# Causal mask of an attention on VectorE, in place of matmuls with the identity

## The chip, the cores and the metric

The kernel is one launch on one core of a Trainium2 chip. The core has TensorE (PE, with a weight load, PEld, ahead of each matmul), VectorE (DVE), ScalarE (ACT), GpSimd (POOL) and SyncE (SP, which issues most of the DMAs here). The metric is the device time of one execution in microseconds; smaller is better. The median of three runs of the kernel before is 1168.8 us (1168.61 to 1170.69).

## The reference

One decoder block on 512 tokens of width 1024 in float32: a SwiGLU half step, a mixing stage, and a second SwiGLU half step. The mixing stage holds a gated MLP over chunks, and a causal differential attention with 8 heads, each with two maps (m = 0, 1) of query and key dimension 64. This is the part that the change touches:

```python
s = jnp.einsum('bhmqd,bhmkd->bhmqk', qb, kf)        # qb: 128 queries, already times 64 ** -0.5
mask = kpos[None, :] <= qpos[:, None]
p = jax.nn.softmax(jnp.where(mask, s, -jnp.inf), axis=-1)
a = p[:, :, 0] - lam * p[:, :, 1]
return jnp.einsum('bhqk,bhkd->bhqd', a, vf)
```

## The kernel before

Activations lie feature by token in tiles of 128 partitions by 512 tokens. Every float32 product is made of three matmuls on operands that are split in two parts: ScalarE casts a tile to the fp32r part `hi` and VectorE subtracts it from the tile to get `lo` (`split`, L138 to L140). Weights come in 512 KB loads on the SP queue into `w_raw`, are split into `w_hi` and `w_lo` (three buffers each in the mixing stage), and each of these chunks feeds one "unit" of 24 matmuls of 512 columns. `pump(n)` runs n units, and starts the load and the split of the next one ahead of the matmuls of the present one.

Between the two SwiGLU parts the program runs a fixed sequence of steps, one for each head h and each block i of 128 queries, 32 in all. A step is `scores(h, i)`, then `pump` of 0 to 2 units by the table `UNITS`, then jobs of earlier steps: `turn_weights` of the step two before (`LAG = 2`) transposes the weights of the softmax and splits them into `at_hi` and `at_lo`, `attend` multiplies them with the values at the end of a head, `mean_square` and `subnorm` normalize the result, `turn` transposes the queries and keys of the next heads, `gate_values` does the gated MLP. The order on each engine is then set by a scheduler that works with costs of its own, so what is written as one step is interleaved with its neighbours.

`scores(h, i)` works on w = 128 (i + 1) keys, so on tiles of 128 by 128 up to 128 by 512. Each map takes one PSUM bank of the pool `att`, which has four; all the transposes, `attend`, `mean_square` and `gate_values` use the same four. Per map there are two matmuls of w columns (L669, L670: the two halves of the contraction hold the parts of queries and keys) and one of 128 columns (L671) that multiplies the identity `ident_r` with the mask `mask_r` and adds -2^100 above the diagonal of the last block. VectorE then takes the negated maximum of each row (L676), ScalarE takes the exponential out of PSUM with this as bias, and the row's sum with it (L677). Reciprocal, scaling and the difference of the two maps follow on VectorE and ScalarE (L680 to L683), in SBUF tiles of the pool `scratch`, which has six.

The two constants are made in `mixing_constants`, which is run inside the first SwiGLU part. The same function scales `qk_col`, the column by which `turn` multiplies the queries.

Of the kernel before, what the change touches and what calls it, by code (L numbers as in the profile page):

```python
# [13 lines left out]
F32 = mybir.dt.float32  # L14
F32R = mybir.dt.float32r
I32 = mybir.dt.int32
AF = mybir.ActivationFunctionType
ALU = mybir.AluOpType
AX = mybir.AxisListType

P = 128
T = 512
# [8 lines left out]
QK = 64  # L31
# [2 lines left out]
LN_EPS = 1e-5  # L34
LAM_INIT = 0.8 - 0.6 * math.exp(0.0)
ROPE_THETA = 500000.0
MASK = -(2.0**100)
RINT = 12582912.0
TWO_PI_A = 6.28125
TWO_PI_B = 2029.0 / 2**20  # L40
# [18 lines left out]
def decoder_block(  # L59
# [25 lines left out]
    nc = tc.nc  # L85
# [6 lines left out]
    small = ctx.enter_context(tc.tile_pool(name="small", bufs=4))  # L92
# [3 lines left out]
    def bank(pool=acc):  # L96
        return pool.tile([P, T], F32, name="bank_" + pool.name, tag=pool.name)
# [7 lines left out]
    def scratch():  # L105
        return tmp.tile([P, T], F32, name="scratch", tag="scratch")
# [37 lines left out]
    ident = const.tile([P, P], F32, name="ident")  # L144
# [257 lines left out]

    mc = ctx.enter_context(tc.tile_pool(name="mc", bufs=1))
    nr = ROT // 2
    ident_r = mc.tile([P, P], F32R, name="ident_r")
    mask_r = mc.tile([P, P], F32R, name="mask_r")
    sub_gain = mc.tile([P, 1], F32, name="sub_gain")
    qk_col = mc.tile([P, 2], F32, name="qk_col")
    neg_lam = mc.tile([P, 1], F32, name="neg_lam")
# [2 lines left out]
    rot2 = mc.tile([P, NT, 2, 2, nr], F32, name="rot2")  # L412

    def mixing_constants():
        nc.vector.tensor_copy(ident_r, ident)
        mask = scratch()[:, :P]
        nc.gpsimd.memset(mask, 0.0)
        nc.gpsimd.affine_select(
            out=mask, in_=mask, compare_op=ALU.is_ge, fill=MASK, base=0, pattern=[[-1, P]], channel_multiplier=1
        )  # L420
        nc.vector.tensor_copy(mask_r, mask)
        c = 3 * KD
        nc.vector.tensor_scalar(sub_gain, gains[:, c : c + 1], LAM_INIT - 1.0, None, op0=ALU.mult)
        nc.vector.tensor_copy(qk_col, gains[:, c + 1 : c + 3])
        nc.vector.tensor_scalar(qk_col[:, 0:1], qk_col[:, 0:1], QK**-0.5, None, op0=ALU.mult)


        s = scratch()
        lam = s[:, : 4 * QK].rearrange("p (a b d) -> p a b d", a=2, b=2)
        lp = s[:, 4 * QK : 6 * QK].rearrange("p (n d) -> p n d", d=QK)  # L430
        le = s[:, 6 * QK : 6 * QK + 2]
        nc.gpsimd.dma_start(out=s[:, : 4 * QK].rearrange("p (n d) -> p n d", d=QK), in_=lam_row.partition_broadcast(P))
        nc.vector.tensor_tensor(lp, lam[:, :, 0, :], lam[:, :, 1, :], op=ALU.mult)
        nc.vector.tensor_reduce(le, lp, axis=AX.X, op=ALU.add)
        nc.scalar.activation(le, le, AF.Exp)
        nc.vector.tensor_tensor(neg_lam, le[:, 1:2], le[:, 0:1], op=ALU.subtract)
        nc.vector.tensor_scalar(neg_lam, neg_lam, -LAM_INIT, None, op0=ALU.add)


        s = scratch()  # L440
        n = NT * nr
        ang, turn, red, sin, cos = (
            s[:, i * n : (i + 1) * n].rearrange("p (t d) -> p t d", d=nr) for i in range(5)
        )
        gain = s[:, 5 * n : 5 * n + 2 * ROT].rearrange("p (q d) -> p q d", d=ROT)
        pos_f = s[:, 7 * n : 7 * n + NT]
        pos_i = small.tile([P, NT], I32, name="pos_i")
        nc.gpsimd.dma_start(out=pos_i, in_=pos)
        nc.gpsimd.dma_start(out=gain, in_=qk_row.partition_broadcast(P))
        nc.vector.tensor_copy(pos_f, pos_i)  # L450
        for i in range(nr):
            inv = float(np.float32(ROPE_THETA ** (-2.0 * i / ROT)))
            nc.vector.tensor_scalar(ang[:, :, i], pos_f, inv, None, op0=ALU.mult)
        for dst, quarter in ((sin, 0.0), (cos, 0.25)):
            nc.vector.tensor_scalar(turn, ang, 1.0 / (2.0 * math.pi), quarter, op0=ALU.mult, op1=ALU.add)
            nc.vector.tensor_scalar(turn, turn, RINT, None, op0=ALU.add)
            nc.vector.tensor_scalar(turn, turn, -RINT, None, op0=ALU.add)
            nc.vector.scalar_tensor_tensor(red, turn, -TWO_PI_A, ang, op0=ALU.mult, op1=ALU.add)
            nc.vector.scalar_tensor_tensor(red, turn, -TWO_PI_B, red, op0=ALU.mult, op1=ALU.add)
            nc.vector.scalar_tensor_tensor(red, turn, -TWO_PI_C, red, op0=ALU.mult, op1=ALU.add)  # L460
            if quarter:
                nc.vector.tensor_scalar(red, red, math.pi / 2.0, None, op0=ALU.add)
            nc.vector.tensor_scalar(red, red, PI32, -PI32, op0=ALU.min, op1=ALU.max)
            nc.scalar.activation(dst, red, AF.Sin)
        for q in range(2):
            g1 = gain[:, q, 0:nr].unsqueeze(1).to_broadcast([P, NT, nr])
            g2 = gain[:, q, nr:ROT].unsqueeze(1).to_broadcast([P, NT, nr])
            nc.vector.tensor_tensor(rot1[:, :, 0, q, :], cos, g1, op=ALU.mult)
            nc.vector.tensor_tensor(rot1[:, :, 1, q, :], sin, g1, op=ALU.mult)
            nc.vector.tensor_tensor(rot2[:, :, 0, q, :], sin, g2, op=ALU.mult)  # L470
            nc.vector.tensor_tensor(rot2[:, :, 1, q, :], cos, g2, op=ALU.mult)


    with tc.tile_pool(name="ff1", bufs=1) as ff1:
        xt = [residual.tile([P, T], F32, name=f"x0_{j}", tag="x") for j in range(KD)]

        def load1(k):
            nc.sync.dma_start(out=xt[k], in_=x[:, k, :])
            normed_input(k, xt[k], 0)

        def prepare1():
            nc.vector.tensor_scalar(neg_gains, gains[:, : 3 * KD], -1.0, None, op0=ALU.mult)
            for j in range(KD):
                add_squares(j, xt[j], latest["hi"])
            norm_scale()

        def constants1():
            with tc.issue_after(latest["hi"].ins), tc.issue_after(latest["lo"].ins):
                mixing_constants()

        def finish1(j, y):
            normed_input(j, y, 1)
            add_squares(j, y)
            nc.gpsimd.dma_start(out=x1_dram[j], in_=y)

        def again1(t, i):
            nc.sync.dma_start(out=t, in_=x[:, 2 * i : 2 * i + 2, :])

        ffn(ff1, gu1, dn1, 0, xt, finish1, load1, {0: prepare1, 5: constants1}, again1)
# [3 lines left out]
    with ExitStack() as mix:  # L503
        half = mix.enter_context(tc.tile_pool(name="half", bufs=PIECES))
        big = mix.enter_context(tc.tile_pool(name="big", bufs=1))

        def piece(name, dtype=F32R):
            return half.tile([P, T], dtype, name=name, tag="piece")
# [152 lines left out]
        heads_out = {}  # L661

        def scores(h, i):
            qd, ql, kd = turned[h]
            w = (i + 1) * P
            qs = slice(i * P, w)
            s = [bank(att)[:, :w] for _ in range(2)]
            for m in range(2):
                nc.tensor.matmul(s[m], lhsT=qd[m][:, qs], rhs=kd[m][:, :w], start=True, stop=False)  # L669
                nc.tensor.matmul(s[m], lhsT=ql[m][:, qs], rhs=kd[m][:, :w], start=False, stop=False)  # L670
                nc.tensor.matmul(s[m][:, qs], lhsT=ident_r, rhs=mask_r, start=False, stop=True)  # L671
            nmx = small.tile([P, 2], F32, name="nmx")
            den = small.tile([P, 2], F32, name="den")
            p = [scratch() for _ in range(2)]
            for m in range(2):
                nc.vector.tensor_reduce(nmx[:, m : m + 1], s[m], axis=AX.X, op=ALU.max, negate=True)  # L676
                nc.scalar.activation(  # L677
                    p[m][:, :w], s[m], AF.Exp, bias=nmx[:, m : m + 1], accum_out=den[:, m : m + 1]
                )
            nc.vector.reciprocal(den, den)  # L680
            nc.vector.tensor_tensor(den[:, 1:2], den[:, 1:2], neg_lam, op=ALU.mult)
            nc.scalar.activation(p[1][:, :w], p[1][:, :w], AF.Copy, scale=den[:, 1:2])
            nc.vector.scalar_tensor_tensor(  # L683
                p[0][:, :w], p[0][:, :w], den[:, 0:1], p[1][:, :w], op0=ALU.mult, op1=ALU.add
            )
            probs[h, i] = p[0]
# [252 lines left out]
        for step in range(max(jobs) + 1):  # L939
            if step < H * NT:  # L940
                scores(*divmod(step, NT))
                pump(UNITS[step // 8][step % 8])
            for work in jobs.get(step, []):
                work()
# [102 lines left out]
```

## Time and profile before

| | us |
|---|---|
| median of three runs | 1168.8 |
| lowest, highest run | 1168.61, 1170.69 |
| the profiled execution | 1167.13 |
| its span on the core | 1165.4 |
| steps of the attention | about 445 to 700 of the span |

The profile is of one execution. Its span goes from the first instruction to the last; 1.7 us of the execution lie around it. PE busy time is the union of matmuls whose ends are modelled and which overlap, so the share of 99% does not say that no time is lost between matmuls; for that one looks at the starts of matmuls that follow one another. A group of instructions has a line of the kernel, an engine, the tile written and the tiles read, and the idle time of that engine just before them with what ended it.

### The profile page before, as it was taken

The page shows a single profiled execution, that of the slowest core. Times are in us where ns is not written, and L with a number is a line of the kernel's source. Part 1 is how long each engine was busy: PE and PEld are TensorE (multiplying, and loading weights), DVE is VectorE, ACT ScalarE, POOL GpSimd, SP SyncE. Part 2 cuts the span into 40 slices and gives each one's busy share as a digit, 9 for nine tenths or more (in the row PEclk, how much of TensorE's full clock was granted, in tenths as well). Part 3 has the DMA queues.
Part 4 walks back from the last instruction along what each step waited for, and adds up shares of the span by engine and source line. Part 5 has one row for each costly group of instructions (what it writes and reads, how often), then busy time and mean ns, then how long its engine had stood idle before and what let it go on. Part 6 is the DMA issues. An engine that isn't in the chain of part 4 may idle for free.

```text
span 1165.4 us, 16669 instructions
## 1 busy us (share of the span) xinstructions
PE 1153.1 (99%) x6618; PEld 1002.2 (86%) x6618; DVE 836.8 (72%) x1294; ACT 589.6 (51%) x856; POOL 29.7 (3%) x58
## 2 busy tenths in 40 slices
PE   8999999999999999999999999999999999999998
PEld 6898899989987888888878778888899899988996
DVE  6985489647786777866778976555788269855875
ACT  7553356415444544567587966333545335523440
POOL 0000000000002000000000001000000000000000
PEclk9999999999999999999999999999999999999999
DMA  8144133413434323122212124334524223431241
GB/s 281 46 132 140 55 115 91 146 55 108 152 111 147 125 69 95 56 91 73 73 55 82 46 73 148 106 109 149 176 73 136 82 73 109 128 119 62 83 154 73
DMA packets 46030, 122.09 MB, mean 105 GB/s; under 512 B 4352, under 2 KB 5408, under 8 KB 45952
## 3 DMA queue, kind: packets, MB, share of 16 engines
q1 hardware_dynamic: 43488, 113.26, 31.0%
q0 software_dynamic: 2464, 7.77, 1.9%
q8 instruction: 52, 0.85, 0.3%
q14 instruction: 26, 0.21, 0.1%
HBM read 114.72 MB, written 6.29 MB: 104 GB/s over the span
## 4 chain that ended last, share of the span: by engine, by line
PE 94%; ACT 2%; DVE 2%; DMA 1%; issue 0%; SPq 0%; DVEq 0%; ACTq 0%
PE bank_acc L324 20%; PE bank_att L324 11%; PE bank_acc L127 11%; PE bank_acc L125 11%; PE bank_acc L126 11%; PE bank_att L127 5%; PE bank_att L126 5%; PE bank_att L125 5%; PE bank_acc L542 4%; PE bank_acc L541 4%; PE bank_acc L540 4%; PE bank_att L669 1%; DMA x<-in_x 1%; PE bank_att L670 1%; PE bank_att L695 1%
## 5 line engine op out<-in xcount | busy, mean ns | idle before, releaser
L139 ACT CAST w_hi<-w_raw 128x1024 fp32r<-128x1024 f32 (+2 forms) x192 | 192.3, 1006 | 288.3 <-PE bank_acc L126 95.5
L140 DVE TENSOR_TENSOR w_lo<-w_raw,w_hi 128x1024 fp32r<-128x1024 f32 (+2 forms) x192 | 223.5, 1167 | 77.2 <-ACT w_hi L139 71.9
L139 ACT CAST w_hi<-w_sum 128x1024 fp32r<-128x1024 f32 x72 | 75.5, 1052 | 142.3 <-PE bank_acc L324 63.6
L324 PE MATMUL bank_acc<-s_lo,w_hi 128*128 128x256 f32 x432 | 121.6, 281 | 0.0
L324 PE MATMUL bank_acc<-s_hi,w_hi 128*128 128x256 f32 x432 | 121.5, 281 | 0.0
L324 PE MATMUL bank_acc<-s_hi,w_lo 128*128 128x256 f32 x432 | 121.4, 281 | 0.0
L140 DVE TENSOR_TENSOR w_lo<-w_sum,w_hi 128x1024 fp32r<-128x1024 f32 x72 | 87.8, 1222 | 27.7 <-ACT w_hi L139 27.7
L125 PE MATMUL bank_acc<-xg_hi,w_hi 128*128 128x512 f32 x224 | 89.3, 399 | 2.1 <-ACT w_hi L139 2.1
L127 PE MATMUL bank_acc<-xg_hi,w_lo 128*128 128x512 f32 x224 | 89.0, 397 | 1.2 <-DVE w_lo L140 1.2
L540 PE MATMUL bank_acc<-w_hi,xg_hi 128*128 128x512 f32 x224 | 89.6, 400 | 0.0
L126 PE MATMUL bank_acc<-xg_lo,w_hi 128*128 128x512 f32 x224 | 88.9, 397 | 0.1
L541 PE MATMUL bank_acc<-w_lo,xg_hi 128*128 128x512 f32 x224 | 88.7, 396 | 0.0
L542 PE MATMUL bank_acc<-w_hi,xg_lo 128*128 128x512 f32 x224 | 88.6, 396 | 0.0
L324 PEld LDWEIGHTS bank_acc<-s_hi,w_lo 128*128 128x128 f32 x432 | 81.7, 189 | 0.0
L324 PEld LDWEIGHTS bank_acc<-s_hi,w_hi 128*128 128x128 f32 x432 | 81.7, 189 | 0.0
L324 PEld LDWEIGHTS bank_acc<-s_lo,w_hi 128*128 128x128 f32 x432 | 81.6, 189 | 0.0
L125 PE MATMUL bank_att<-a_hi,w_hi 128*128 128x512 f32 x176 | 69.4, 394 | 0.0
L125 PE MATMUL bank_acc<-a_hi,w_hi 128*128 128x512 f32 x176 | 69.4, 394 | 0.0
L126 PE MATMUL bank_att<-a_lo,w_hi 128*128 128x512 f32 x176 | 69.4, 394 | 0.0
L126 PE MATMUL bank_acc<-a_lo,w_hi 128*128 128x512 f32 x176 | 69.4, 394 | 0.0
L127 PE MATMUL bank_acc<-a_hi,w_lo 128*128 128x512 f32 x176 | 69.4, 394 | 0.0
L127 PE MATMUL bank_att<-a_hi,w_lo 128*128 128x512 f32 x176 | 69.4, 394 | 0.0
(271 smaller groups left out, 2859.5 us busy)
## 6 DMA issues: line engine op xcount, KB each, us to landing
w_raw<-in_gu SPq DMA_DIRECT2D x86, 512.0 KB, 3.8
w_raw<-in_dn SPq DMA_DIRECT2D x32, 512.0 KB, 3.5
w_raw<-in_w_qk SPq DMA_DIRECT2D x16, 512.0 KB, 3.7
w_raw<-in_dn SPq DMA_DIRECT2D x16, 384.0 KB, 3.4
w_raw<-in_w_v SPq DMA_DIRECT2D x8, 512.0 KB, 3.6
w_raw<-in_w_ga SPq DMA_DIRECT2D x8, 512.0 KB, 3.6
w_raw<-in_w_gb SPq DMA_DIRECT2D x8, 512.0 KB, 3.7
w_raw<-in_w_pb SPq DMA_DIRECT2D x8, 512.0 KB, 3.6
```

The costliest lines, as they stand in the source:

```text
L125: nc.tensor.matmul(ps, lhsT=lhi, rhs=rhi, start=first, stop=False)
L126: nc.tensor.matmul(ps, lhsT=lhi, rhs=rlo, start=False, stop=False)
L127: nc.tensor.matmul(ps, lhsT=llo, rhs=rhi, start=False, stop=last)
L139: latest["hi"] = nc.scalar.copy(hi, src)
L140: latest["lo"] = nc.vector.tensor_tensor(lo, src, hi, op=ALU.subtract)
L324: nc.tensor.matmul(o, lhsT=l[:, s], rhs=r, start=first and f == kt == i == 0, stop=kt == HK - 1 and i == 2, skip_group_check=True,)
L540: nc.tensor.matmul(banks[t], lhsT=xg_hi[k][:, ts], rhs=hi[:, s], start=k == 0, stop=False)
L541: nc.tensor.matmul(banks[t], lhsT=xg_hi[k][:, ts], rhs=lo[:, s], start=False, stop=False)
L542: nc.tensor.matmul(banks[t], lhsT=xg_lo[k][:, ts], rhs=hi[:, s], start=False, stop=k == KD - 1)
L669: nc.tensor.matmul(s[m], lhsT=qd[m][:, qs], rhs=kd[m][:, :w], start=True, stop=False)
L670: nc.tensor.matmul(s[m], lhsT=ql[m][:, qs], rhs=kd[m][:, :w], start=False, stop=False)
L695: nc.tensor.transpose(ps[:, j * P : (j + 1) * P], a[:, j * P : (j + 1) * P], ident)
```

## The change

The matmuls with the identity go, and with them the tiles `ident_r` and `mask_r` and what fills them. In their place there is one tile `mask` of 128 by 512 in SBUF, which GpSimd fills at the start of the mixing stage; its last w columns are the mask of a tile of w keys. The queries are negated (by the sign in `qk_col`), so PSUM holds -s. One VectorE instruction per map, `tensor_tensor_reduce`, reads PSUM and the mask, writes -s + mask to a `scratch` tile in SBUF and keeps the minimum of each row; a second small instruction, which the call issues with it, writes this minimum out to `low`. ScalarE then takes the exponential in place in SBUF, with scale -1 and the minimum as bias.

```diff
-MASK = -(2.0**100)
+MASK = 2.0**100
...
-    ident_r = mc.tile([P, P], F32R, name="ident_r")
-    mask_r = mc.tile([P, P], F32R, name="mask_r")
...
-        nc.vector.tensor_copy(ident_r, ident)
-        mask = scratch()[:, :P]
-        nc.gpsimd.memset(mask, 0.0)
-        nc.gpsimd.affine_select(
-            out=mask, in_=mask, compare_op=ALU.is_ge, fill=MASK, base=0, pattern=[[-1, P]], channel_multiplier=1
-        )
-        nc.vector.tensor_copy(mask_r, mask)
...
-        nc.vector.tensor_scalar(qk_col[:, 0:1], qk_col[:, 0:1], QK**-0.5, None, op0=ALU.mult)
+        nc.vector.tensor_scalar(qk_col[:, 0:1], qk_col[:, 0:1], -(QK**-0.5), None, op0=ALU.mult)
...
+        mask = big.tile([P, T], F32, name="mask")
+        nc.gpsimd.memset(mask, 0.0)
+        nc.gpsimd.affine_select(
+            out=mask, in_=mask, compare_op=ALU.is_ge, fill=MASK, base=T - P, pattern=[[-1, T]], channel_multiplier=1
+        )
...
-                nc.tensor.matmul(s[m], lhsT=ql[m][:, qs], rhs=kd[m][:, :w], start=False, stop=False)
-                nc.tensor.matmul(s[m][:, qs], lhsT=ident_r, rhs=mask_r, start=False, stop=True)
-            nmx = small.tile([P, 2], F32, name="nmx")
+                nc.tensor.matmul(s[m], lhsT=ql[m][:, qs], rhs=kd[m][:, :w], start=False, stop=True)
+            low = small.tile([P, 2], F32, name="low")
...
-                nc.vector.tensor_reduce(nmx[:, m : m + 1], s[m], axis=AX.X, op=ALU.max, negate=True)
+                pm = p[m][:, :w]
+                nc.vector.tensor_tensor_reduce(
+                    pm, s[m], mask[:, T - w :], 1.0, 2.0 * MASK, ALU.add, ALU.min, accum_out=low[:, m : m + 1]
+                )
                 nc.scalar.activation(
-                    p[m][:, :w], s[m], AF.Exp, bias=nmx[:, m : m + 1], accum_out=den[:, m : m + 1]
+                    pm, pm, AF.Exp, scale=-1.0, bias=low[:, m : m + 1], accum_out=den[:, m : m + 1]
                 )
```

The change also moves instructions, since the scheduler sets the order anew. First PE, at the scores of head 1 with 512 keys (`k` and `q` are its keys and queries, `ya` operands of a unit, `sq` those of `mean_square`). Before:

```order
2970 L125 MATMUL bank_acc<-ya_hi_4383,w_hi 128x512
2971 L669 MATMUL bank_att<-k_0_3923,q_0_3906 128x512
2972 L670 MATMUL bank_att<-k_0_3923,ql_0_3908 128x512
2973 L671 MATMUL bank_att<-mask_r,ident_r 128x128
2974 L126 MATMUL bank_acc<-ya_lo_4384,w_hi 128x512
2975 L127 MATMUL bank_acc<-ya_hi_4383,w_lo 128x512
2976 L125 MATMUL bank_acc<-ya_hi_4427,w_hi 128x512
2977 L126 MATMUL bank_acc<-ya_lo_4428,w_hi 128x512
2978 L669 MATMUL bank_att<-k_1_3924,q_1_3907 128x512
2979 L670 MATMUL bank_att<-k_1_3924,ql_1_3909 128x512
2980 L671 MATMUL bank_att<-mask_r,ident_r 128x128
2981 L127 MATMUL bank_acc<-ya_hi_4427,w_lo 128x512
```

The same place on PE in the changed kernel, where L666 and L667 are the two matmuls of the scores and L718 is that of `mean_square`:

```order
2956 L125 MATMUL bank_acc<-ya_hi_4377,w_hi 128x512
2957 L666 MATMUL bank_att<-k_0_3919,q_0_3902 128x512
2958 L667 MATMUL bank_att<-k_0_3919,ql_0_3904 128x512
2959 L126 MATMUL bank_acc<-ya_lo_4378,w_hi 128x512
2960 L127 MATMUL bank_acc<-ya_hi_4377,w_lo 128x512
2961 L125 MATMUL bank_acc<-ya_hi_4419,w_hi 128x512
2962 L126 MATMUL bank_acc<-ya_lo_4420,w_hi 128x512
2963 L127 MATMUL bank_acc<-ya_hi_4419,w_lo 128x512
2964 L666 MATMUL bank_att<-k_1_3920,q_1_3903 128x512
2965 L667 MATMUL bank_att<-k_1_3920,ql_1_3905 128x512
2966 L125 MATMUL bank_acc<-ya_hi_4497,w_hi 128x512
2967 L718 MATMUL bank_att<-sq_hi_4929,ones_r 128x512
```

The two mask matmuls are gone; the second map stands one matmul of the unit later, and `mean_square` stands earlier than it did. Second, DVE at the scores of head 0 with 512 keys. Before:

```order
488 L676 TENSOR_REDUCE nmx<-bank_att 128x1
489 L823 TENSOR_TENSOR scratch<-scratch,u_3838 128x512
490 L676 TENSOR_REDUCE nmx<-bank_att 128x1
491 L140 TENSOR_TENSOR w_lo<-w_raw,w_hi 128x1024
492 L140 TENSOR_TENSOR ya_lo_4508<-scratch,ya_hi_4507 128x512
493 L680 RECIPROCAL den<-den 128x2
494 L681 TENSOR_TENSOR den<-den,neg_lam 128x1
495 L683 SCALAR_TENSOR_TENSOR scratch<-scratch,den 128x512
```

The same place on DVE in the changed kernel (the new instruction is listed as ISA, by the line of the call):

```order
491 L673 ISA scratch,low<-bank_att,mask 128x512
492 L673 ISA low 128x1
493 L822 TENSOR_TENSOR scratch<-scratch,u_3834 128x512
494 L673 ISA scratch,low<-bank_att,mask 128x512
495 L673 ISA low 128x1
496 L140 TENSOR_TENSOR w_lo<-w_raw,w_hi 128x1024
497 L140 TENSOR_TENSOR ya_lo_4498<-scratch,ya_hi_4497 128x512
498 L679 RECIPROCAL den<-den 128x2
```

Each reduction has become two instructions on VectorE, in the same place ahead of the split of a weight chunk.

## Rows read from the trace of the kernel before

**Rows 1.** The page: busy time, share of the span and instructions of each engine.

```profile
PE 1153.1 (99%) x6618; PEld 1002.2 (86%) x6618; DVE 836.8 (72%) x1294; ACT 589.6 (51%) x856; POOL 29.7 (3%) x58
```

**Rows 2.** Stretches: length, busy us of PE, PEld, DVE, ACT, POOL (instructions), clock, DMA, GB/s.

```profile
300.00:400.00 100.00, 100.00 (x528) 84.60 (x527) 77.09 (x130) 49.55 (x64) 11.22 (x18) 1.00 0.42 137
...
445.00:700.00 255.00, 252.41 (x1259) 207.45 (x1258) 197.18 (x456) 178.63 (x352) 6.25 (x12) 1.00 0.23 69
640.00:670.00 30.00, 29.37 (x146) 23.53 (x145) 27.25 (x53) 28.45 (x57) 1.04 (x2) 1.00 0.16 51
```

**Rows 3.** Waits of PE, 440 to 720 us: us in total, times, longest.

```profile
PE bank_att L669 <- ACT scratch L677: 0.7, 2, 0.4
PE bank_att L695 <- ACT scratch L677: 0.6, 2, 0.4
PE bank_att L719 <- ACT sq_hi L139: 0.5, 1, 0.5
PE bank_att L669 <- ACT ms L721: 0.4, 1, 0.4
```

**Rows 4.** PE in order of time: start, duration (us), line, tiles; 512 keys, then 128.

```profile
546.93 0.39 PE L670 MATMUL bank_att<-k,ql 128*128 128x512 f32 x1
547.16 0.22 PE L671 MATMUL bank_att<-mask_r,ident_r 128*128 128x128 f32 x1
547.22 0.44 PE L669 MATMUL bank_att<-k,q 128*128 128x512 f32 x1
547.51 0.39 PE L670 MATMUL bank_att<-k,ql 128*128 128x512 f32 x1
547.74 0.22 PE L671 MATMUL bank_att<-mask_r,ident_r 128*128 128x128 f32 x1
...
449.01 0.27 PE L671 MATMUL bank_att<-mask_r,ident_r 128*128 128x128 f32 x1
449.12 0.27 PE L669 MATMUL bank_att<-k,q 128*128 128x128 f32 x1
449.24 0.28 PE L670 MATMUL bank_att<-k,ql 128*128 128x128 f32 x1
```

**Rows 5.** DVE groups by line, 445 to 700 us: busy, mean ns, idle before.

```profile
L676 DVE TENSOR_REDUCE nmx<-bank_att 128x1 f32<-128x128 f32 (+3 forms) x64 | 30.3, 485 | 6.6 <-PE bank_att L671 6.2
L683 DVE SCALAR_TENSOR_TENSOR scratch<-scratch,den 128x128 f32<-128x128 f32 (+3 forms) x32 | 17.6, 549 | 9.4 <-ACT scratch L682 9.2
L140 DVE TENSOR_TENSOR at_lo<-bank_att,at_hi 128x128 fp32r<-128x128 f32 (+3 forms) x32 | 15.5, 487 | 0.6 <-ACT at_hi L139 0.5
L681 DVE TENSOR_TENSOR den<-den,neg_lam 128x1 f32<-128x1 f32 x32 | 5.0, 157 | 0.8
```

**Rows 6.** DVE groups, shapes apart, 445 to 700 us.

```profile
L676 DVE TENSOR_REDUCE nmx<-bank_att 128x1 f32<-128x512 f32 x16 | 10.8, 682 | 0.5 <-PE bank_att L671 0.5
...
L676 DVE TENSOR_REDUCE nmx<-bank_att 128x1 f32<-128x128 f32 x16 | 4.4, 283 | 0.2
```

**Rows 7.** DVE in order of time: a small instruction and the next one.

```profile
664.88 0.16 DVE L680 RECIPROCAL den<-den 128x2 f32<-128x2 f32 x1
664.95 0.67 DVE L855 TENSOR_TENSOR ga<-ga,bank_acc 128x512 f32<-128x512 f32 x1
```

**Rows 8.** ACT groups by line, 445 to 700 us.

```profile
L677 ACT ACTIVATE scratch<-bank_att,nmx 128x128 f32<-128x128 f32 (+3 forms) x64 | 33.7, 530 | 23.6 <-DVE nmx L676 22.6 <-DVE den L681 0.7
L682 ACT ACTIVATE scratch<-scratch,den 128x128 f32<-128x128 f32 (+3 forms) x32 | 18.1, 564 | 13.7 <-DVE den L681 13.5
L677 ACT ACTIVATION_READ_ACCUMULATOR scratch<-bank_att,nmx 128x1 f32 x64 | 12.8, 201 | 0.0
```

**Rows 9.** DVE, first step: end of its softmax; PE line L695, 445 to 480 us.

```profile
453.72 0.35 DVE L683 SCALAR_TENSOR_TENSOR scratch<-scratch,den 128x128 f32<-128x128 f32 x1 [0.53 <-ACT scratch L682]
...
L695 PE MATMUL bank_att<-ident,scratch x3: 272/272/273, 466.1 to 474.5; 128*128 128x128 f32 x3
```

**Rows 10.** POOL in order of time, start of the mixing stage.

```profile
361.85 0.54 POOL L494 DMA_DIRECT2D x_dram<-y  x1 [3.79 <-DVE y L397]
365.33 0.54 POOL L782 DMA_DIRECT2D w_raw<-in_ws  x1 [2.94 <-DVE w_lo L140]
369.05 2.17 POOL L784 TENSOR_SCALAR_AFFINE_SELECT w_raw<-w_raw 128x1024 f32<-128x1024 f32 x1 [3.17 <-DMA w_raw<-in_ws]
```

## The prediction

> **What bounds the kernel now.** I read the busy times first: PE is busy for 99% of the span, DVE for 72%, ACT for 51% [rows 1]. Then the stretches: in the steps of the attention, 445 to 700 us, PE is busy for 252.4 of 255 us at full granted clock (1.00), DVE for 197.2 (77%) and ACT for 178.6 (70%) [rows 2]. Then PE's waits there: four kinds, 2.2 us in all, of which 1.3 us are for banks that the exponential L677 had not yet left [rows 3]. So PE sets the end, in this stage too, and what it no longer has to issue comes off the time, as long as DVE and ACT keep up. They have less room in one place: from 640 to 670 us DVE is busy for 27.25 and ACT for 28.45 of 30 us [rows 2].
>
> **What goes from PE.** 64 matmuls (8 heads, 4 blocks, 2 maps) and their weight loads. Their duration of 0.22 to 0.27 us is no price, since they overlap with their neighbours; the price is read from starts [rows 4]. With 512 keys L671 starts at 547.16 and the next matmul at 547.22: 0.06 us. But that one then takes until 547.51, 0.29 us, while the same shape without a mask matmul in front takes 0.23 (546.93 to 547.16, and 547.51 to 547.74). So 0.06 + 0.06 = 0.12 us go with it. With 128 keys the mask matmul takes 449.01 to 449.12, 0.11 us, and the matmuls behind it take as much each, mask in front or not. I take 0.11 for all: 64 x 0.11 = 7.0 us. The bounds are 64 x 0.06 = 3.8 us, if the second half is not given back, and 64 x 0.22 = 14.1 us by durations, which overlapping starts contradict.
>
> A rule of the Trainium skill stands beside this. The page "TensorE: Matmul & The Clock Gate", section "Back-to-back issue gap", gives about 81 ns for each 128-column matmul in a stream of weight loads and matmuls. By it the term is 64 x 0.081 = 5.2 us, an estimate from that page, and the time would be 1.8 us above the one I forecast; the starts here, 0.11 us apart, do not agree, and I keep them.
>
> **What is added on DVE.** 64 reductions of 485 ns on average [rows 5] become 64 instructions that read PSUM and SBUF and write SBUF, and 64 that write the minimum out. The trace has neither. For the first the nearest row is the subtraction into `at_lo`: one source in PSUM, one in SBUF, result in SBUF, the same four shapes, 487 ns; the next is L683, which has a third operand, 549 ns [rows 5]. For the second the rows are the smallest DVE instruction, 157 ns [rows 5], the read of ACT's accumulator, 201 ns [rows 8], and the 0.07 us from the start of a small instruction to that of the next [rows 7]. Per tile this gives 0.002 + 0.07 = 0.07 us at the least and 0.064 + 0.201 = 0.27 at the most of near rows; I take 0.002 + 0.157 = 0.16, because the `at_lo` row has the same operands. Below nothing it can hardly be: the same elements pass, and an instruction is added. Above, a rate of half an element in place of one is the far end: the reduction's slope is (682 - 283) / 384 = 1.04 ns per element [rows 6], so at 320 elements on average 0.33 more, 0.49 us with the second instruction. In total 10 us for my value, 4 to 31 us by the bounds, on an engine that has 255 - 197 = 58 us free in the stage, 51 after PE's gain.
>
> What that costs is decided where DVE is nearly full. From 640 to 670 us five steps run, ten tiles; PE's 30 us become 28.9, DVE's 27.25 become 27.25 + 10 x 0.16 = 28.85. It just fits, and ACT (28.45, see below) is as close. By the near upper bound it is 27.25 + 2.7 = 29.95, 1.05 us too long; with a few stretches as dense, some 3 us. I take 1.0 us of new waits of PE, between 0 and 3. Queued behind the new instruction on DVE are the splits of weight chunks, for which the units' matmuls wait; these have buffers for about one unit ahead.
>
> The chain through one step gets longer: two reads of the minimum in a row, 0.3 us, before the exponential. It is hidden: the first step's weights are ready at 454.07, and the first transposes (L695) start at 466.1 [rows 9], 12 us later.
>
> **What moves to SBUF on ACT.** The exponential reads SBUF and not PSUM. ACT from SBUF to SBUF with the same shapes (L682) takes 564 ns against 530 for L677 [rows 8]: 64 x 0.034 = 2.2 us on an engine with 76 us free in the stage; nothing on the path, except in the dense stretch, where it adds 0.3 us to ACT's 28.45 and stays below 28.9. In return the bank is free when DVE has passed it, not when the exponential has: the 1.3 us of PE's waits for L677 [rows 3] should go. What is late next there are the splits and squares, 0.9 us, which stay. The `scratch` tile is taken earlier, by DVE; six of them and a softmax that ends 12 us before its transposes leave room.
>
> **Constants.** Two casts of 128 x 128 on DVE and two GpSimd instructions leave the first SwiGLU part, where PE is busy for 100.0 of 100 us [rows 2]: 0. The mask tile is filled on POOL ahead of the load of the gate's weights (L782). POOL is free from 362.4 to 365.33; the select of 1024 columns takes 2.17 us, so 512 about 1.1, and with the fill some 1.7 [rows 10]: it ends at 364.1 and nothing moves. If the tile's memory came free later, the load L782 would be late by up to 1.7 us, and PE, with 100 of 100 us busy there and the gate's products due at 455 us, would not see it. 0, and half a microsecond at most.
>
> **Sum.** -7.0 - 1.3 + 1.0 = -7.3 us. The profiled execution, 1167.1 us (span 1165.4 and 1.7 around it), would take 1159.8; it stands 1.7 below the median of the runs, so the median goes from 1168.8 to 1161.5.
>
> **Rivals.**
> - More (PE's idle goes as well): all 2.2 us of waits go and nothing is added, and the price of a mask matmul is 0.12: 7.7 + 2.2 = 9.9, 1158.9, or lower still. For it: banks come free earlier. Against: the waits L719 do not depend on that.
> - Less: only the start of the next matmul, 0.06 us, is won, or DVE's near upper bound holds: -7.0 - 1.3 + 3 = -5.3, or -3.8 - 1.3 + 1.0 = -4.1: 1163.5 to 1164.7. Against the first: 0.29 against 0.23 us in rows 4.
> - No change: DVE and ACT, both full from 640 to 670 us, pass their delay on through the steps, since the scheduler's order was made with its own costs for an instruction that the trace does not have. It takes 7 us of new waits, so 1168.8 less about 1, some 1167.5. For it: both engines end within 0.1 us of PE in my own sum. Against: 51 us of free DVE time in the stage, and a unit's worth of buffers.
> - Slower: the new instruction runs at half rate, 0.49 us more per tile, and DVE becomes the bound of the dense stretches. From 640 to 670 us it is 27.25 + 4.9 = 32.2 us against PE's 28.9, 3.3 too long; DVE over the whole stage goes to 197 + 31 = 228 of 248 us, 92%, so I count the same again for some four stretches, 13 us: -7.0 - 1.3 + 13 = +5, 1173.5. It decides from about 0.35 to 0.45 us more per tile on. Against: `at_lo`, two sources at 487 ns, is as quick as the reduction with one.
>
> The Trainium skill has a rule on that side: "Vector Engine (DVE) Microarchitecture Reference", section "Points that are easy to get wrong", says that an instruction of the two-source layout with an accumulator halves its throughput when both sources are in SBUF and wider than bf16. No run here shows the new instruction; L683, two float32 sources in SBUF, at 549 ns is far from twice 485, and the new one has a source in PSUM, so by rule and rows I leave this rival low.
>
> **Chances.** Forecast, -9 to -5.5 us: 0.57. More: 0.09. Less, -5.5 to -2.3: 0.15. No change: 0.10. Slower: 0.09. A measurement of this kernel tells about 0.2%, 2.3 us, from nothing: faster 0.81, within 0.2% 0.10, slower 0.09. The range, 1157 to 1167.5, holds the forecast, nearly all of "more", all of "less" and the lower part of no change, some 8 to 9 in 10.
>
> **What would show it.** Right: in the same stage 64 PE instructions fewer and the stage 7 us shorter, the matmul behind the scores' last at 0.23 us; no PE wait for the exponential; DVE's new pair at about 0.49 and 0.16 us mean, DVE busy some 207 us in the stage; the time outside the stage as before. Wrong: a mean of the new instruction above 0.8 us; PE waits for `w_lo`, or for the transposes' weights, of more than 3 us in all; or a stage shortened by only 4 us with no new waits, which would put the price of a mask matmul at its start-to-start time.

## The result, and the profile after

The changed kernel takes 1159.07 us (median of six runs, 1156.86 to 1160.05) against 1168.7 us for the kernel before on the same chip (six runs, 1167.02 to 1170.69): ratio 0.9917, interval 0.9904 to 0.993, which is 9.6 us less, between 8 and 11. Two more sets of runs gave 0.9913 (0.99 to 0.9927) and 0.9912 (0.9899 to 0.9926). The forecast was 1161.5, in a range of 1157.0 to 1167.5: faster, as forecast, by 9.6 us in place of 7.3.

The profiled execution took 1159.7 us, with a span of 1158.0. The page's first line, busy us of each engine, for the changed kernel:

```profile
PE 1146.5 (99%) x6554; PEld 996.1 (86%) x6554; DVE 836.4 (72%) x1356; ACT 590.0 (51%) x856; POOL 30.5 (3%) x58
```

Beside [rows 1], PE has 64 instructions and 6.6 us less, VectorE 62 instructions more and no more busy time. Where the time went is read best from three starts on PE: the first matmul of L324 (in the first SwiGLU part), the first of the scores, and the first of L324 in the second SwiGLU part. These are the rows of the kernel before (start, duration, line):

```profile
54.64 0.28 PE L324 MATMUL bank_acc<-xg_hi,w_hi 128*128 128x256 f32 x1
...
448.84 0.22 PE L669 MATMUL bank_att<-k,q 128*128 128x128 f32 x1
...
858.16 0.28 PE L324 MATMUL bank_acc<-xg_hi,w_hi 128*128 128x256 f32 x1
```

And those of the changed kernel:

```profile
56.83 0.28 PE L324 MATMUL bank_acc<-xg_hi,w_hi 128*128 128x256 f32 x1
...
451.03 0.22 PE L666 MATMUL bank_att<-k,q 128*128 128x128 f32 x1
...
850.74 0.28 PE L324 MATMUL bank_acc<-xg_hi,w_hi 128*128 128x256 f32 x1
```

From the first to the second it is 394.20 us in both. From the second to the third it is 409.32 before and 399.71 after: 9.61 us less. This stretch, from the first scores to the second SwiGLU part, is called the stage below; it is the same within 0.1 us in all three profiles of the changed kernel (399.71, 399.64, 399.69). The start of the launch took 2.2 us more in this one execution (56.83 against 54.64), which is why the two profiled executions differ by 7.4 us and the medians by 9.6.

Inside the stage, these are PE's starts at scores with 512 keys in the changed kernel, the place of [rows 4]:

```profile
545.78 0.48 PE L666 MATMUL bank_att<-k,q 128*128 128x512 f32 x1
546.10 0.40 PE L667 MATMUL bank_att<-k,ql 128*128 128x512 f32 x1
546.33 0.39 PE L666 MATMUL bank_att<-k,q 128*128 128x512 f32 x1
546.56 0.39 PE L667 MATMUL bank_att<-k,ql 128*128 128x512 f32 x1
546.79 0.40 PE L536 MATMUL bank_acc<-w_hi,xg_hi 128*128 128x512 f32 x1
547.02 0.39 PE L537 MATMUL bank_acc<-w_lo,xg_hi 128*128 128x512 f32 x1
```

In the kernel before, the first and the last matmul of the same place are these:

```profile
546.62 0.48 PE L669 MATMUL bank_att<-k,q 128*128 128x512 f32 x1
...
548.09 0.40 PE L541 MATMUL bank_acc<-w_lo,xg_hi 128*128 128x512 f32 x1
```

The second map follows at 0.23 us and the unit behind it at 0.23: the 0.06 us of the mask matmul and the 0.06 us that it laid on the next one are both gone. PE's waits in the stage, which were four kinds and 2.2 us [rows 3], are now 0.6 us (us in total, times, longest):

```profile
PE bank_att L694 <- DVE k L649: 0.2, 1, 0.2
PE bank_att L666 <- DVE low L673: 0.2, 1, 0.2
PE bank_att L666 <- DVE at_lo L140: 0.2, 1, 0.2
```

On VectorE, the groups that answer to [rows 5] (busy, mean ns, idle before):

```profile
L673 DVE CUSTOM_DVE_ANT_0 scratch<-bank_att,mask 128x128 f32<-128x128 f32 (+3 forms) x64 | 29.8, 485 | 5.4 <-PE bank_att L667 4.8
...
L673 DVE DVE_READ_ACCUMULATOR2_ANT low<- 128x1 f32 x64 | 5.3, 83 | 0.0
```

The fused instruction takes what the plain reduction took, 485 ns, though it reads a second operand and writes a tile; reading the minimum out takes 83 ns. These are durations, and on VectorE too they overlap. At the scores above, the two reductions before and the two pairs after stand like this (start, duration):

```profile
547.42 1.29 DVE L676 TENSOR_REDUCE nmx<-bank_att 128x1 f32<-128x512 f32 x2 [0.21 <-PE bank_att L671]
548.63 0.68 DVE L140 TENSOR_TENSOR sq_lo<-scratch,sq_hi 128x512 fp32r<-128x512 f32 x1
...
546.53 0.69 DVE L673 CUSTOM_DVE_ANT_0 scratch<-bank_att,mask 128x512 f32<-128x512 f32 x1 [0.17 <-PE bank_att L667]
547.15 0.08 DVE L673 DVE_READ_ACCUMULATOR2_ANT low<- 128x1 f32 x1
547.15 0.69 DVE L673 CUSTOM_DVE_ANT_0 scratch<-bank_att,mask 128x512 f32<-128x512 f32 x1
547.76 0.08 DVE L673 DVE_READ_ACCUMULATOR2_ANT low<- 128x1 f32 x1
547.76 0.69 DVE L140 TENSOR_TENSOR sq_lo<-scratch,sq_hi 128x512 fp32r<-128x512 f32 x1
```

The next instruction starts together with the read of the minimum, at 547.15 and at 547.76. From the first start to that of the split it is 1.21 us before and 1.23 after, so a pair costs VectorE about 0.01 us more than a reduction, and its busy time in the stage does not grow (length, then busy us of PE, PEld, DVE, ACT, POOL; before, then after):

```profile
448.84:858.16 409.32, 406.73 (x1923) 331.84 (x1922) 294.18 (x584) 247.96 (x444) 14.85 (x28) 1.00 0.29 91
451.03:850.74 399.71, 398.94 (x1859) 324.61 (x1858) 293.42 (x648) 248.58 (x444) 14.84 (x28) 1.00 0.29 93
```

On ScalarE, beside [rows 8]:

```profile
L676 ACT ACTIVATE scratch<-scratch,low 128x128 f32<-128x128 f32 (+3 forms) x64 | 35.7, 562 | 15.0 <-DVE low L673 14.3 <-DVE rt L160 0.3
```

The exponential takes 562 ns from SBUF, 32 ns more than from PSUM, and waits less for VectorE (14.3 us against 22.6). The mask tile is filled on GpSimd where it was idle, beside [rows 10]:

```profile
364.55 0.55 POOL L498 MEMSET mask<- 128x512 f32 x1
365.17 1.17 POOL L499 TENSOR_SCALAR_AFFINE_SELECT mask<-mask 128x512 f32<-128x512 f32 x1
367.71 0.56 POOL L781 DMA_DIRECT2D w_raw<-in_ws  x1 [1.37 <-DVE w_lo L140]
```

It ends at 366.34, and the load behind it still waits for something else (a split on VectorE) until 367.71.

### The profile page after: what moved, and what is told of

The parts are those of the page before. It is cut to its first block, busy times and chain, and to the rows that moved or that the text cites. A ratio compares the mean times of both kernels' runs of the same rounds, so it can differ in the third digit from the quotient of the medians.

```text
span 1158.0 us, 16621 instructions
## 1 busy us (share of the span) xinstructions
PE 1146.5 (99%) x6554; PEld 996.1 (86%) x6554; DVE 836.4 (72%) x1356; ACT 590.0 (51%) x856; POOL 30.5 (3%) x58
## 4 chain that ended last, share of the span: by engine, by line
PE 95%; ACT 2%; DVE 1%; DMA 1%; issue 0%; SPq 0%; DVEq 0%; ACTq 0%
PE bank_acc L324 20%; PE bank_att L324 11%; PE bank_acc L127 11%; PE bank_acc L125 11%; PE bank_acc L126 11%; PE bank_att L127 5%; PE bank_att L126 5%; PE bank_att L125 5%; PE bank_acc L536 4%; PE bank_acc L538 4%; PE bank_acc L537 4%; DMA x<-in_x 1%; PE bank_att L666 1%; PE bank_att L667 1%; PE bank_att L694 1%
## 5 line engine op out<-in xcount | busy, mean ns | idle before, releaser
L324 PE MATMUL bank_acc<-s_lo,w_hi 128*128 128x256 f32 x432 | 121.6, 281 | 0.0
L324 PE MATMUL bank_acc<-s_hi,w_hi 128*128 128x256 f32 x432 | 121.5, 281 | 0.0
L324 PE MATMUL bank_acc<-s_hi,w_lo 128*128 128x256 f32 x432 | 121.4, 281 | 0.0
L324 PEld LDWEIGHTS bank_acc<-s_hi,w_lo 128*128 128x128 f32 x432 | 81.7, 189 | 0.0
L324 PEld LDWEIGHTS bank_acc<-s_hi,w_hi 128*128 128x128 f32 x432 | 81.7, 189 | 0.0
L324 PEld LDWEIGHTS bank_acc<-s_lo,w_hi 128*128 128x128 f32 x432 | 81.6, 189 | 0.0
```

The lines of the kernel that those rows point to most:

```text
L324: nc.tensor.matmul(o, lhsT=l[:, s], rhs=r, start=first and f == kt == i == 0, stop=kt == HK - 1 and i == 2, skip_group_check=True,)
```

## The experiments

The theory was that the matmuls' slots on PE make the greater part of the gain, and the banks that come free earlier a small part. The rival: the banks make it, and the matmuls were hidden. Since the stage repeats within 0.1 us, each run is judged by it as well as by its time. Every edit also makes the scheduler set the order of PE's instructions anew, so a difference of the stage holds the edit and its new order together.

| run | time, us | ratio to before (interval) | stage, us |
|---|---|---|---|
| before | 1167.7 to 1168.7 | 1 | 409.32 |
| changed kernel, three sets | 1159.07, 1158.38, 1157.71 | 0.9917, 0.9913, 0.9912 | 399.71, 399.64, 399.69 |
| zero matmuls put back | 1167.21 | 0.9992 (0.9983 to 1.0001) | 408.24 |
| before, no mask at all | 1160.43 | 0.9926 (0.9913 to 0.9938) | 400.98 |
| exponential from PSUM again | 1159.37 | 0.9927 (0.9914 to 0.9939) | 400.91 |
| second fused pass | 1160.57 | 0.9934 (0.9921 to 0.9948) | 402.25 |
| three fused passes | 1171.44 | 1.003 (1.002 to 1.0041) | 412.88 |
| two zero matmuls per map | 1174.47 | 1.0056 (1.0044 to 1.0069) | 416.12 |
| matmuls of half the rows | 1164.05 | 0.9966 (0.9955 to 0.9976) | 405.73 |

**The base.** The changed kernel twice more.

> The changed kernel unaltered, on the same chip as the three others, as the base for their differences. Theory and rival alike: 1159 us, within 1.5, so 9 to 10 us under the kernel before. If the start of the launch (0 to 60 us) took 2.2 us more in its first profile by chance, the stretch before 60 us is back near that of the kernel before in at least some runs here.

Measured: 1158.38 us, 9.4 under the kernel before; its first L324 stood at 54.23, so the late start in the first profile was of that execution. The third set:

> The changed kernel unaltered, as the base on this chip: 1158.4 to 1159.1 us, and from its first scores to the second SwiGLU part 402.5 us as in its two profiles so far.

Measured: 1157.71 us, and 399.69 us by the starts of the table (402.5 in the text counts to a matmul 2.8 us further on); here the start was late again, 57.19.

**The matmuls put back.**

```diff
+        nc.vector.tensor_copy(ident_r, ident)
+        nc.vector.memset(zero_r.bitcast(F32), 0.0)
...
-                nc.tensor.matmul(s[m], lhsT=ql[m][:, qs], rhs=kd[m][:, :w], start=False, stop=True)
+                nc.tensor.matmul(s[m], lhsT=ql[m][:, qs], rhs=kd[m][:, :w], start=False, stop=False)
+                nc.tensor.matmul(s[m][:, qs], lhsT=ident_r, rhs=zero_r, start=False, stop=True)
```

> The changed kernel with the 64 matmuls of 128 columns with the identity put back on PE, now against a tile of zeros, so that the mask still comes from VectorE. Theory (PE's issue slots make the greater part of the gain, 0.11 to 0.12 us each): 64 x 0.115 = 7.4 us slower than the changed kernel, 1166.4, and the first matmul behind each at 0.28 to 0.29 us again. Rival (the gain comes from PSUM banks that are free before the exponential, and the matmuls were hidden): within 2 us of the changed kernel, 1159 to 1161.

Measured: 1167.21 us, 8.8 above the changed kernel on that chip, and the stage 8.6 longer than the mean of the changed kernel's. The gain is back with the matmuls, so the rival falls; of the whole change without their removal 0.6 us are left by the times, not told from nothing, and 1.08 by the stage. The rows show the old pattern (start, duration, line):

```profile
548.39 0.22 PE L672 MATMUL bank_att<-zero_r,ident_r 128*128 128x128 f32 x1
548.45 0.44 PE L670 MATMUL bank_att<-k,q 128*128 128x512 f32 x1
548.73 0.39 PE L671 MATMUL bank_att<-k,ql 128*128 128x512 f32 x1
```

0.06 us, and then 0.28 for 512 columns. PE's waits at banks are 1.4 us here; none is for the exponential, but others have come up (the same view as above):

```profile
PE bank_att L670 <- ACT ms L725: 0.8, 2, 0.5
PE bank_att L723 <- ACT sq_hi L139: 0.4, 1, 0.4
PE bank_att L670 <- DVE low L678: 0.2, 1, 0.2
```

**The matmuls alone taken away.**

```diff
-                nc.tensor.matmul(s[m], lhsT=ql[m][:, qs], rhs=kd[m][:, :w], start=False, stop=False)
-                nc.tensor.matmul(s[m][:, qs], lhsT=ident_r, rhs=mask_r, start=False, stop=True)
+                nc.tensor.matmul(s[m], lhsT=ql[m][:, qs], rhs=kd[m][:, :w], start=False, stop=True)
```

> The kernel before without its 64 mask matmuls and with nothing in their place: the causal mask is left out. Reduction and exponential read PSUM as before, VectorE does nothing more than before. Theory: 7.0 to 7.4 us under the kernel before, 1161.4, with PE's waits for banks held by the exponential (1.3 to 2.2 us) still there. Rival (banks): within 2 us of the kernel before, 1167 to 1169. If VectorE's and ScalarE's additions cost the changed kernel something, this one is below it, under 1159.

Measured: 1160.43 us, 7.4 under the kernel before, and the stage 8.34 shorter. That is the theory's size, and a little more by the stage. The waits did not stay as expected: for the exponential only 0.2 us are left, though it still reads PSUM:

```profile
PE bank_att L669 <- ACT ms L720: 0.5, 1, 0.5
PE bank_att L694 <- ACT scratch L676: 0.2, 1, 0.2
```

So most of these waits went with the matmuls and the order that came of it, and not because the bank was freed by another engine. This run and the one with zeros put back give all four corners: the matmuls cost 8.34 us of the stage with the old softmax and 8.6 with the new one; the new softmax gains 1.08 us with the matmuls and 1.3 without. The two add up.

**The bank alone.**

```diff
-                    pm, pm, AF.Exp, scale=-1.0, bias=low[:, m : m + 1], accum_out=den[:, m : m + 1]
+                    pm, s[m], AF.Exp, scale=-1.0, bias=low[:, m : m + 1], accum_out=den[:, m : m + 1]
```

> The changed kernel with the exponential reading the bank in PSUM again; VectorE still does the fused pass and writes its SBUF tile, which the exponential then overwrites. So the mask is left out of the exponential (it stays in the minimum), a bank is held until the exponential has passed, and ScalarE's read is the shorter one (530 against 562 ns). It tells apart what lies between the changed kernel and the kernel before without mask matmuls (1.3 us of the stage). Theory (the early release of banks is worth 1.3 us): 1.3 us above the changed kernel, about 1159.7, as that one, and VectorE's 83 ns more per tile cost nothing. Rival (banks are worth more, and VectorE's addition takes part of it back): 2.5 us or more above the changed kernel, over 1160.9. Second rival (banks are worth nothing): within 0.5 us of it.

Measured: 1159.37 us, 1.7 above the changed kernel on that chip with intervals that overlap; the stage says 1.2 us above it, and 0.07 below the run without a mask. So what the new softmax gains goes when the bank is held longer, and VectorE's read of the minimum, 83 ns by its duration, costs nothing that shows. How the 1.2 us come about is open: PE's named waits here are 0.7 us and none is for the exponential, and PE's order differs from the changed kernel's within the first sixty matmuls of the stage, so an early bank may act by the waits or by the order. The exponential is at 530 ns again; what ScalarE's longer read costs lies inside the 1.2 us and was not measured by itself.

**How much room VectorE has.** A second pass over the tile in SBUF; the run after it has two of them, in a loop, with 8.0 * MASK as the start of the minimum.

```diff
+                nc.vector.tensor_tensor_reduce(
+                    pm, pm, mask[:, T - w :], 1.0, 2.0 * MASK, ALU.add, ALU.min, accum_out=low[:, m : m + 1]
+                )
```

> The changed kernel with a second fused instruction behind each first one, which reads the SBUF tile just written and the mask, adds the mask again and takes the minimum again: 64 more passes and 64 more reads of the minimum, some 0.49 + 0.08 us per tile, 36 us more on VectorE, 230 of 245 us in the stage. Theory of the prediction (VectorE decides from 0.35 to 0.45 us more per tile on, by its dense stretches): 3 to 13 us slower than the changed kernel, 1162 to 1172. Rival (only VectorE's total counts, and it has 50 us free): within 1.5 us, 1159 to 1160.5. Beside it: by the rule that two wide sources in SBUF with an accumulator halve the throughput the second pass lasts 0.8 us on average, otherwise 0.49 as the first; at 0.8 VectorE would have 250 us of work in the stage and the time would be over 1170.

Measured: 1160.57 us, 2.2 above the changed kernel, the stage 2.6 longer. It lies between the two theories: one more pass costs 2.6, less than the prediction's rule gave. The 36 us in the expectation are durations. By starts a pass with its read takes VectorE 0.21 us at 128 columns and 0.61 at 512, 0.41 on average and 26 us in all, and VectorE's busy time in the stage rises by 23.1 us, from 293.42 to 316.55 (first this run, then the one with three passes):

```profile
448.87:851.12 402.25, 400.43 (x1860) 323.91 (x1858) 316.55 (x776) 249.44 (x444) 14.81 (x28) 1.00 0.29 92
449.59:862.47 412.88, 404.48 (x1860) 326.07 (x1858) 339.17 (x904) 249.35 (x444) 14.80 (x28) 0.99 0.28 90
```

The second pass has two float32 sources in SBUF, the first one in PSUM:

```profile
L676 DVE CUSTOM_DVE_ANT_0 scratch<-scratch,mask 128x128 f32<-128x128 f32 (+3 forms) x64 | 30.4, 484 | 0.2
L673 DVE CUSTOM_DVE_ANT_0 scratch<-bank_att,mask 128x128 f32<-128x128 f32 (+3 forms) x64 | 30.2, 484 | 1.5 <-PE bank_att L667 1.3
```

Both take 484 ns, so the half rate of the prediction's slower rival does not appear in either form. The Trainium skill ("Vector Engine (DVE) Microarchitecture Reference", "Points that are easy to get wrong") says of one instruction layout with an accumulator that two SBUF sources that are not bf16 halve its throughput. The 484 ns do not show this; whether the instruction used here has that layout, no run shows.

> The changed kernel with two more fused passes per tile, so three in all. From the run with one more: 0.484 + 0.083 us per pass and tile, 36 us per pass on VectorE. VectorE's work in the stage is then some 194 + 73 = 267 us against PE's 245, so it must be the bound. Theory (VectorE's total decides, its dense stretches little): 20 to 30 us slower than the changed kernel, 1179 to 1188. By the prediction's rule (dense stretches decide from about 0.4 us per tile on, some four of them): more than that, over 1190. If it is under 1170, VectorE has more room than its busy time says.

Measured: 1171.44 us, 13.1 above the changed kernel by the medians of two sets, the stage 13.2 longer: outside both expectations, below the lower one (20 to 30) and above 1170. The waits turn from banks to splits of weights (PE's longest over the whole span):

```profile
PE bank_acc L127 <- DVE w_lo L140: 6.3, 4, 2.5
```

Of these, 1.2 us lie outside the stage, in the kernel before too. Behind two of the others PE's granted clock falls, which it does in the stage of no other profile here (length, busy us of PE, PEld, DVE, ACT, POOL, clock):

```profile
655.00:665.00 10.00, 8.07 (x27) 6.04 (x28) 8.46 (x24) 7.37 (x13) 0.00 (x0) 0.83 0.36 107
720.00:730.00 10.00, 7.51 (x27) 5.68 (x26) 10.00 (x16) 2.52 (x5) 0.00 (x0) 0.86 0.17 51
```

Matmuls of 512 columns then start 0.42 to 0.43 us apart in place of 0.23:

```profile
659.12 0.63 PE L125 MATMUL bank_acc<-ya_hi,w_hi 128*128 128x512 f32 x1
659.54 0.63 PE L126 MATMUL bank_acc<-ya_lo,w_hi 128*128 128x512 f32 x1
```

That is the lower level, 1.2 of 2.4 GHz. At some eight such matmuls each time it makes about 3 us of the 13.2, an estimate from these starts; the rest is waits. VectorE is busy for 238.10 of 255 us from 445 to 700 us and for 339.17 of 412.88 in the stage, so its total comes near the limit without reaching it; it is full in stretches, as from 720 to 730 us above, where PE is busy for 7.51 of 10. One pass more, 0.41 us per tile by starts, costs 2.6 us, and two, 0.82 us, cost 13.2.

**The price of a matmul, by doubling.** The run with zeros put back, with the zero matmul issued twice per map.

```diff
+                nc.tensor.matmul(s[m][:, qs], lhsT=ident_r, rhs=zero_r, start=False, stop=False)
                 nc.tensor.matmul(s[m][:, qs], lhsT=ident_r, rhs=zero_r, start=False, stop=True)
```

> The changed kernel with two matmuls of 128 columns with the identity and zeros per map, 64 more than in the run that put one back. By starts a matmul costs 0.114 us, by the difference of the stage 0.134. If only slots count: 7.3 us above the run with one, some 1174.5. If each brings waits along as the first did: 8.6 us above, some 1176.

Measured: 1174.47 us, 7.3 above the run with one by the medians of two sets; the stage 7.88 longer, 0.123 us for each. It lies at the slots' price by the times and between the two by the stage: beyond 0.115 us per slot, a matmul brings at most a little along (PE's named waits rise from 1.4 to 2.4 us).

**A version meant to be faster.**

```diff
-                nc.gpsimd.memset(ql[m][other].bitcast(F32), 0.0)
...
             for m in range(2):
-                nc.tensor.matmul(s[m], lhsT=qd[m][:, qs], rhs=kd[m][:, :w], start=True, stop=False)
-                nc.tensor.matmul(s[m], lhsT=ql[m][:, qs], rhs=kd[m][:, :w], start=False, stop=True)
+                both = nc.tensor.matmul(s[m], lhsT=qd[m][:, qs], rhs=kd[m][:, :w], start=True, stop=False)
+            for m in range(2):
+                own = slice(m * QK, (m + 1) * QK)
+                both = in_turn(
+                    nc.tensor.matmul(s[m], lhsT=ql[m][own, qs], rhs=kd[m][own, :w], start=False, stop=True), both
+                )
```

> A version meant to beat the changed kernel in the same way, by fewer PE slots. Of the second matmul of each map (the small part of the queries) half of the 128 rows are zeros; here only the 64 rows that count are used, rows 0 to 63 for the first map and 64 to 127 for the second, and the two matmuls stand behind one another, 32 pairs, each into its own bank. GpSimd's fills with zeros go. Theory one (the two run in the array at once): 32 x 0.16 us on average over the four widths = 5.1 us under the changed kernel, 1153.3. Theory two (they go one after the other): within 1.5 us of it, 1158.4.

Measured: 1164.05 us, slower than the changed kernel by some 6 us (stage 6.0), so the times of both theories fall. The rows at scores with 512 keys (x2 is the pair):

```profile
467.47 0.47 PE L665 MATMUL bank_att<-k,q 128*128 128x512 f32 x1
467.87 0.50 PE L669 MATMUL bank_att<-k,ql 64*128 64x512 f32 x2
468.30 0.50 PE L537 MATMUL bank_acc<-w_lo,xg_hi 128*128 128x512 f32 x1
468.63 0.39 PE L538 MATMUL bank_acc<-w_hi,xg_lo 128*128 128x512 f32 x1
```

Two rows of one line are merged here; the same line by itself, in the first 0.01 us of the pair, shows both matmuls at work (length, busy us and count of PE, of PEld):

```profile
467.87:467.88 0.01, 0.01 (x2) 0.01 (x2) 1.00 0.99 410
```

In all 32 pairs the second starts 3 to 4 ns behind the first, so the two do run at once, as theory one says. But from the pair's start to the next matmul it is 0.43 us (467.87 to 468.30), where two matmuls of full height take 0.46, and the neighbours take longer: the one ahead 0.40 us in these rows and 0.32 to 0.33 in the other seven pairs of this width, the one behind 0.33, where such matmuls take 0.23 in the changed kernel's rows above. So 0.03 us are won and some 0.2 lost at 512 columns. Why a matmul next to a pair takes longer is not settled; no version here beats the changed kernel.

## Why the prediction was right

**The bound and the stage.** Right: PE decides in the stage, and the two long stretches on either side kept their time: 394.20 us ahead of it in both, and 301.63 behind it in both (from the third start to that of PE's last matmul, 858.16 to 1159.79 and 850.74 to 1152.37).

**The matmuls' slots.** The mechanism was right and the size a little short: -7.0 us forecast, -8.34 to -8.6 measured, 0.130 to 0.134 us for each in place of 0.11. About 7.4 are the slots: with 512 keys the rows run from the first score matmul to the second of the unit in 1.47 us before (546.62 to 548.09) and 1.24 after (545.78 to 547.02), 0.115 us for each of two. The lower bound (the second half not given back) and the upper one (durations) are both out. The remaining 1 us went with the waits: without the mask matmuls and with nothing else changed, PE's named waits in the stage fall from 2.2 to 0.7 us. By which of its steps one matmul less lets a bank come free earlier was not traced.

By the 81 ns per matmul that the Trainium skill gives ("TensorE: Matmul & The Clock Gate", "Back-to-back issue gap") the term would have been 5.2 us, an estimate from that page; the measured 0.130 us is further from it than the 0.11 of the forecast was.

**The banks.** -1.3 us forecast; 1.08 to 1.3 us measured, by two differences of the stage, and the run in which only the bank is held longer gives 1.2. But the reading was not as clean as the size: the waits in [rows 3] that I put down to the exponential went for the greater part with the matmuls, and with the matmuls put back the wait moved to other releasers. The size came out near the sum of those waits by luck: no run shows the gain to be made of them.

**VectorE's addition.** The term that was furthest off for its size: +1.0 us forecast for new waits, none that shows measured. I took a whole small instruction, 157 ns, for the read of the minimum, and 0.07 us as the least. It lasts 83 ns, but by starts the pair costs VectorE only 0.01 us more than the reduction did, so even my lower bound was too high. I had priced PE by starts and VectorE by durations. The dense stretch was thus hardly tested by the change: from 640 to 670 us VectorE is busy for 27.30 us, where 28.85 were forecast:

```profile
640.00:670.00 30.00, 29.85 (x149) 24.22 (x148) 27.30 (x62) 28.96 (x56) 0.00 (x0) 1.00 0.16 52
```

The runs with more passes test it. One pass adds 0.41 us per tile by starts, which lies in the 0.35 to 0.45 from which I said that VectorE decides, and it does cost something, but 2.6 us, where I reckoned 13 for 0.49 and the same sum gives some 10 for 0.41. So where VectorE begins to count was not wrong; that each of four stretches passes its whole overflow, 3.3 us, on to PE was.

**What was costed at nothing.** Right for the constants and the mask tile on GpSimd: the time ahead of the stage is the same, 394.20 us. Nothing speaks against it for the longer chain through a step (PE's waits after the change name no transposes that lack their weights of the softmax) and for the longer read on ScalarE, but neither was tested alone.

**The sum.** -7.0 - 1.3 + 1.0 = -7.3 became -8.4 - 1.2 + 0 = -9.6. The measured time is inside the stated range, but outside the -9 to -5.5 us to which I gave 0.57. It came out near the rival "more" (-9.9, given 0.09), and in part for its reasons: nothing was added, more waits went, and a matmul was worth more than 0.11 us. The two larger misses, of the matmuls and of VectorE, go the same way, so neither covered the other. The other rivals fall: "less" by the rows, "no change" and "slower" by the runs with more passes.

## What to carry to other kernels

Where one engine is full, price a small instruction on it by the starts of its neighbours with it and without it, and not by its duration: here 0.22 us of duration on PE were 0.06 us of own slot and 0.06 us laid on the next matmul, and 83 ns on VectorE were about 0.01. The same holds for an engine that is not full when one asks how much room it has. An engine that is 91% busy for a stretch can still have some: add a pass and see what it costs; here 0.41 us more per tile cost 2.6 us and 0.82 cost 13.2. A consumer that copies out of PSUM in the instruction it has to run anyway gives the bank back early; here that was worth 1.1 to 1.3 of 9.6 us, with the order that the scheduler made of it.

## What the runs showed that was not expected

The start of the launch comes in two kinds, for the same kernel too. In profiles whose first matmul of L324 stood at 56.4 to 57.2 us, the granted clock between 20 and 30 us was 0.83; in those where it stood at 54.2 to 55.4, it was 1.00. Two profiles of the changed kernel, first the one at 56.83 (length, busy us of PE, clock, DMA share, GB/s):

```profile
10.00:20.00 10.00, 8.55 (x37) 1.00 1.01 367
20.00:30.00 10.00, 8.73 (x31) 0.83 0.72 229
```

and then the one at 54.23:

```profile
10.00:20.00 10.00, 9.74 (x41) 1.00 0.98 359
20.00:30.00 10.00, 9.27 (x40) 1.00 0.71 227
```

0.83 as a mean of ten microseconds means that for about a third of them the clock stood at the lower of its two levels, 1.2 of 2.4 GHz. Ahead of it the DMA engines are full in both, and PE waits for its first weights; in the first it was idle for more of the ten microseconds from 10 to 20 us, ahead of the fall, 1.45 us against 0.26. The kernel before at 54.64 had been as idle (8.51 of 10) and kept its clock, so this idle time alone does not decide it. The later start is 1 to 3 us behind the earlier one, up to a third of the effect studied here, and of that the lower clock itself can make at most 1.7 us (0.17 of ten). It is why stretches of the trace told more than single times.
